# The first layer of the gate's low-rank path as three fp32r products, their low parts made on GpSimd

## The chip, the cores and the metric

The kernel runs on one core of a Trainium2 chip. Time is device time of one execution in microseconds, the median of several runs. A core has five engines with queues of their own: TensorE (PE in the profile, its weight loads PEld), VectorE (DVE), ScalarE (ACT), GpSimd (POOL) and SyncE (SP, which here issues transfers). They wait for each other at semaphores.

## What is computed

The reference is a decoder trunk of two layers over 272 tokens of 2048 features (16 learned tokens ahead of 256). Layer 0 is an RWKV-7 time mix, layer 1 a stick-breaking attention, each followed by a SwiGLU. What matters here is how the time mix makes its inputs, and one of its low-rank paths, the gate g:

```
xx = token_shift(h) - h
xr, xw, xk, xv, xa, xg = (h + xx * mu[i] for i in range(6))
r, k, v = xr @ w_r, xk @ w_k, xv @ w_v
w = -softplus(-(dec_w0 + tanh(xw @ dec_w1) @ dec_w2)) - 0.5      # dec_w1: 2048 x 96
a = sigmoid(a_w0 + (xa @ a_w1) @ a_w2)                            # a_w1:   2048 x 96
g = sigmoid(xg @ g_w1) @ g_w2                                     # g_w1:   2048 x 256
```

The change concerns the product `xg @ g_w1`.

## The kernel before, in words

Activations lie transposed in SBUF: 16 tiles of 128 features by 272 tokens, numbered k. A matrix product with a 2048-wide input sums over these 16 k in PSUM.

Most products are made in two parts. A float32 tensor is cast by ScalarE to the type fp32r (the high part) and VectorE subtracts the cast from the original (the low part). A product is then three fp32r matmuls, high by high, high weight by low activation and low weight by high activation (`mm3k`, lines 189 to 191). Weights arrive in tiles `raw` by SyncE's queue and are split so, in chunks of 512 columns, into `whi` (line 170) and `wlo` (line 171). A chunk is four k, so 12 matmuls. Four `raw` tiles exist, each with two chunks, and a `raw` is free for the next load when both chunks are split.

The split chunks go by turns into the pool `whl` (six pairs) and, in the prologue, into the pool `wx` (ten tiles, tag "w", that is five pairs).

The prologue normalizes the input (tiles `hn`), makes the key projection w_k for 16 output blocks m, and beside it everything else that needs the mixes. A mix is two instructions: ScalarE makes `u` (line 451), VectorE the mix `xi` (line 452) from hn and u. `u` has three buffers, `xi` seven. The generator `rest()` makes the value mixes, then the first layers of the three low-rank paths, then the mixes for r. From block 4 on, each key projection (`proj`) is followed by the output of the block (`key_out`: copy `kt`, square, cast and low part `hs`, and two matmuls into `kq`, line 528) and by four steps of `rest()`. So four k of the low-rank first layers belong to one key block, and the 16 k take four blocks. In each k, the paths of decay (i = 1) and iclr (i = 4) are one plain float32 matmul, with 96 columns of weights, and the gate (i = 5) two, each with 128 columns (j = 0, 1). All four are line 587 before, and their tiles in PSUM are named `lr`. These weights aren't split: `da` holds dec_w1 and a_w1 of two k, `gg` g_w1 of two k, both loaded by SyncE (line 581).

No order is written by hand here: a scheduler lays out every engine's instructions when the kernel is built, and each engine then takes its own in that order. It put each group of four k as a "burst" a few matmuls behind the start of the next key block. GpSimd does nothing in the prologue; behind it, in the scan, it fills some tiles and solves small triangles.

Of the kernel before, what the change touches and what calls it, by code (L numbers as in the profile page):

```python
# [11 lines left out]
F32 = mybir.dt.float32  # L12
F32R = mybir.dt.float32r
AF = mybir.ActivationFunctionType
ALU = mybir.AluOpType
# [3 lines left out]
NK = D // 128  # L19
META = 16  # L20
SEQ = 256
T = META + SEQ
# [99 lines left out]
class Builder:  # L122
# [286 lines left out]
    def prologue(self, hid):  # L409

        tc, nc, a = self.tc, self.nc, self.a
        V, A = nc.vector, nc.scalar
        with ExitStack() as ctx:
            x0 = ctx.enter_context(tc.tile_pool(name="x0", bufs=NK))
            wx = ctx.enter_context(tc.tile_pool(name="wx", bufs=NWX))
# [8 lines left out]
            def xtile():  # L424
                return pt.tile([128, T], F32, name="xi", tag="xi", bufs=NXL)
# [23 lines left out]
            def mixed(i, k, out):  # L449
                u = pt.tile([128, T], F32, name="u", tag="u", bufs=NSQ)  # L450
                A.mul(u, hn[k][:, :T], self.vec(f"mu{i}", k))
                V.scalar_tensor_tensor(out, hn[k][:, 1:], self.vec(f"om{i}", k), u, ALU.mult, ALU.add)

            def mix(i, k, pool):
                x = xtile()
                mixed(i, k, x)
                if pool is not self.xs2:
                    return self.split(x, pool)
                hi, lo = (pool.tile([128, T], F32R, name=n, tag="s") for n in ("hi", "lo"))
                A.copy(hi, x)  # L460
                V.tensor_tensor(lo, x, hi.bitcast(F32), ALU.subtract)
                return hi, lo
# [3 lines left out]
                                                         tag="mm" if m < 2 else "fr")  # L466
# [12 lines left out]
            for k in range(NK):  # L479
# [4 lines left out]
                x = xtile()  # L484
                mixed(2, k, x)
                for m in range(G0):
                    o = k % 4 * 128
                    nc.tensor.matmul(ps[m][:, :T], w0[m, k // 4][:, o:o + 128], x,  # L488
                                     start=k == 0, stop=k == NK - 1)
# [63 lines left out]
            def hsplit(t, name):  # L553
                m = t.shape[0]
                hi = hid.tile([m, T], F32R, name=name + "h", tag=name + "h")
                lo = hid.tile([m, T], F32R, name=name + "l", tag=name + "l")
                A.copy(hi, t)
                V.tensor_tensor(lo, t, hi.bitcast(F32), ALU.subtract)
                return hi, lo

            def rest():

                for k in range(NK):
                    self.xv.append(mix(3, k, self.xs1))
                    yield 1
                names = ((1, ["dec_w1"]), (4, ["a_w1"]), (5, ["g_w1", "g_w1"]))
                bk = {(i, j): (self.psd if i < 5 else self.pfr).tile(
                    [128, 512], F32, name="lr", tag="sd" if i < 5 else "fr")
                    for i, n in names for j in range(len(n))}
                for k in range(NK):  # L570
                    if k % 2 == 0:
                        w = {}
                        da = self.l2.tile([128, 512], F32, name="raw", tag="w2", bufs=2)
                        gg = self.l2.tile([128, 512], F32, name="raw",
                                          tag="w2h" if k % 4 else "w2l", bufs=1)
                        for (i, j), t, o, c, src in (
                                ((1, 0), da, 0, 96, a["dec_w1"]), ((4, 0), da, 192, 96, a["a_w1"]),
                                ((5, 0), gg, 0, 128, a["g_w1"][0]),
                                ((5, 1), gg, 256, 128, a["g_w1"][1])):
                            w[i, j] = t[:, o:o + 2 * c]  # L580
                            nc.sync.dma_start(w[i, j], src[:, k * c:(k + 2) * c])
                    for i, n in names:
                        x = xtile()
                        mixed(i, k, x)
                        c = 96 if i < 5 else 128
                        for j in range(len(n)):
                            nc.tensor.matmul(bk[i, j][:c, :T], w[i, j][:, k % 2 * c:k % 2 * c + c], x,  # L587
                                             start=k == 0, stop=k == NK - 1)
                    yield 1
                for i, name in ((1, "dec_w1"), (4, "a_w1")):  # L590
                    t = xtile()[:96]
                    if i == 1:
                        A.activation(t, bk[i, 0][:96, :T], AF.Tanh)
                        self.hw = hsplit(t, name)
                    else:
                        A.copy(t, bk[i, 0][:96, :T])
                        self.ha = hsplit(t, name)
                for j in range(2):
                    g = xtile()
                    A.activation(g, bk[5, j][:, :T], AF.Tanh, scale=0.5)  # L600
                    V.tensor_scalar(g, g, 0.5, 0.5, ALU.mult, ALU.add)
                    self.hg.append(hsplit(g, f"hg{j}"))
                yield 1
                for k in range(NK):
                    self.xr.append(mix(0, k, self.xs2))
                    yield 1

            g = rest()
            for m in range(G0, NK):
                key_out(m, self.proj(a["w_k"][m], xk))  # L610
# [903 lines left out]
```

## Time and profile before

| | us |
|---|---|
| median of 3 runs | 2654.6 (2654.39 to 2655.65) |
| the profiled execution | 2656.68 |
| its span, first to last instruction | 2654.9 |
| PE busy in it | 2641.9 |
| VectorE, ScalarE, GpSimd busy | 1787.6, 1490.5, 174.1 |
| the four bursts of line 587 | 82.2 to 130.4 in the span |

A row of the timeline gives start, length, engine, line, operation, out<-in and shapes; instructions of one kind in a row are merged ("x7"), and behind them stands the idle time ahead and what ended it. PE's matmuls are pipelined, so the time between starts is the cost of one, not its length. A float32 matmul stands as two records, an fp32r one as one.

### The profile page before, as it was taken

What the parts mean: (1) busy time and instruction counts of PE and PEld (TensorE: products, weight loads), DVE (VectorE), ACT (ScalarE), POOL (GpSimd) and SP (SyncE); (2) the same over time, 40 slices, a digit from 0 to 9 for tenths busy, and PEclk for the clock granted to TensorE, in tenths of its full rate; (3) what the DMA queues carried; (4) which work ended last, traced back from release to release, by engine and by line L of the source; (5) the groups of instructions that cost most, each with busy time, mean ns of one, the idle gap of its engine ahead of it and who ended that gap; (6) DMA issues with size and microseconds to landing.
All of it is one profiled execution on the core that took longest, in us unless ns stands there. A gap on an engine that the chain in (4) does not pass through costs nothing.

```text
span 2654.9 us, 54070 instructions
## 1 busy us (share of the span) xinstructions
PE 2641.9 (100%) x20966; PEld 2455.2 (92%) x20966; DVE 1787.6 (67%) x3618; ACT 1490.5 (56%) x3017; POOL 174.1 (7%) x493
## 2 busy tenths in 40 slices
PE   9999999999999999999999999999999999999999
PEld 8898888889999999999999999888888888888888
DVE  7677777766655555555557775788766666666665
ACT  7775666666544444444446764676555455554553
POOL 0014343440000000000000000000000000000000
PEclk9999999999999999999999999999999999999999
DMA  6434343445555555555555555434555655665655
GB/s 229 145 120 130 96 127 97 124 132 165 174 175 165 186 175 165 185 176 167 184 174 168 181 167 175 143 120 137 189 187 180 197 188 176 201 190 176 199 180 177
DMA packets 186385, 439.54 MB, mean 166 GB/s; under 512 B 58736, under 2 KB 89616, under 8 KB 186128
## 3 DMA queue, kind: packets, MB, share of 16 engines
q1 hardware_dynamic: 184784, 432.90, 51.9%
q8 instruction: 164, 2.69, 0.4%
q0 software_dynamic: 768, 2.23, 0.3%
q10 hardware_dynamic: 576, 0.96, 0.1%
q14 instruction: 93, 0.76, 0.1%
HBM read 430.28 MB, written 5.74 MB: 164 GB/s over the span
## 4 chain that ended last, share of the span: by engine, by line
PE 97%; DMA 1%; ACT 1%; issue 1%; DVE 0%; POOL 0%; SPq 0%; POOLq 0%; ACTq 0%
PE mm L194 23%; PE mm L189 17%; PE mm L191 17%; PE mm L190 17%; PE mm L193 12%; PE lr L587 1%; PE mm L488 1%; PE cb L1426 1%; PE zb L1363 1%; PE yb L1344 1%; PE wa L1374 1%; PE z L1054 1%; PE cb L1418 0%; PE lt L1067 0%; PE ba L1226 0%
## 5 line engine op out<-in xcount | busy, mean ns | idle before, releaser
L171 DVE TENSOR_TENSOR wlo<-raw,whi 128x512 fp32r<-128x512 f32 (+1 forms) x1432 | 968.0, 679 | 596.4 <-ACT whi L170 576.5
L170 ACT CAST whi<-raw 128x512 fp32r<-128x512 f32 (+1 forms) x1432 | 870.3, 610 | 841.2 <-PE mm L190 531.3
L189 PE MATMUL mm<-hl,whi 128*128 128x272 f32 x3328 | 967.2, 291 | 0.0
L191 PE MATMUL mm<-hl,wlo 128*128 128x272 f32 x3328 | 960.4, 289 | 0.0
L190 PE MATMUL mm<-hl,whi 128*128 128x272 f32 x3328 | 958.1, 288 | 0.0
L194 PE MATMUL mm<-hl,whi 128*128 128x512 f32 x2624 | 919.9, 394 | 0.0
L193 PE MATMUL mm<-hl,wlo 128*128 128x256 f32 x2624 | 738.1, 282 | 0.0
L189 PEld LDWEIGHTS mm<-hl,whi 128*128 128x128 f32 x3328 | 625.3, 188 | 10.7 <-issue 8.1
L190 PEld LDWEIGHTS mm<-hl,whi 128*128 128x128 f32 x3328 | 631.2, 190 | 0.0
L191 PEld LDWEIGHTS mm<-hl,wlo 128*128 128x128 f32 x3328 | 625.6, 188 | 0.2
L194 PEld LDWEIGHTS mm<-hl,whi 128*128 128x128 f32 x2624 | 492.4, 188 | 111.9
L193 PEld LDWEIGHTS mm<-hl,wlo 128*128 128x128 f32 x2624 | 494.3, 188 | 0.3
L218 DVE TENSOR_TENSOR wlo<-raw,whi 128x512 fp32r<-128x512 f32 (+2 forms) x156 | 106.6, 691 | 21.7 <-ACT whi L217 19.3
L217 ACT CAST whi<-raw 128x512 fp32r<-128x512 f32 (+2 forms) x156 | 93.1, 609 | 41.4 <-PE mm L190 40.9
L210 DVE TENSOR_TENSOR h<-h,mm 128x256 f32<-128x256 f32 (+1 forms) x224 | 93.9, 420 | 6.6 <-PE mm L194 6.0
L203 ACT COPY c<-mm 128x256 f32<-128x256 f32 x104 | 38.8, 373 | 75.8 <-PE mm L194 75.8
L1281 POOL TENSOR_TENSOR Ts<-Ts,Tm 40x14 f32<-40x14 f32 (+6 forms) x224 | 76.6, 342 | 17.6
L189 PE MATMUL mm<-hi,whi 128*128 128x272 f32 x256 | 75.5, 295 | 0.0
L1279 POOL TENSOR_TENSOR Tm<-Ts,As 40x14 f32<-40x14 f32 (+6 forms) x224 | 74.3, 331 | 17.5
L190 PE MATMUL mm<-lo,whi 128*128 128x272 f32 x256 | 73.8, 288 | 0.0
L191 PE MATMUL mm<-hi,wlo 128*128 128x272 f32 x256 | 73.4, 287 | 0.0
L189 PEld LDWEIGHTS mm<-hi,whi 128*128 128x128 f32 x256 | 48.0, 188 | 1.1
(295 smaller groups left out, 2365.1 us busy)
## 6 DMA issues: line engine op xcount, KB each, us to landing
raw<-w_gate SPq DMA_DIRECT2D x176, 512.0 KB
raw<-w_up SPq DMA_DIRECT2D x176, 512.0 KB
raw<-w_down SPq DMA_DIRECT2D x128, 512.0 KB
raw<-w_down SPq DMA_DIRECT2D x128, 192.0 KB
raw<-w_v SPq DMA_DIRECT2D x32, 512.0 KB
raw<-w_r SPq DMA_DIRECT2D x32, 512.0 KB
raw<-sb_w_k SPq DMA_DIRECT2D x32, 512.0 KB
raw<-sb_w_v SPq DMA_DIRECT2D x32, 512.0 KB
```

Of the source, the lines that this page charges most:

```text
L170: nc.scalar.copy(hi, part)
L171: nc.vector.tensor_tensor(lo, part, hi.bitcast(F32), ALU.subtract)
L189: mm(out, w[0], x[0], start=first, stop=False)
L190: mm(out, w[0], x[1], start=False, stop=False)
L191: return mm(out, w[1], x[0], start=False, stop=last)
L193: mm(out[:, :n], w[1], x[0], start=first, stop=False, skip_group_check=True)
L194: return mm(out, w[0], x[2], start=False, stop=last, skip_group_check=True)
L210: self.nc.vector.tensor_tensor(h, h, out[:, c:c + n], ALU.add)
L217: self.cast = nc.scalar.copy(hi, part)
L218: nc.vector.tensor_tensor(lo, part, hi.bitcast(F32), ALU.subtract)
L1279: V.tensor_tensor(t, Ts[:, 0:i, i:i + 1].to_broadcast([40, i, n]), As[:, i:i + 1, i + 1:].to_broadcast([40, i, n]), ALU.mult)
L1281: V.tensor_tensor(Ts[:, 0:i, i + 1:], Ts[:, 0:i, i + 1:], t, ALU.add)
```

## The change

The two gate products of each k become six fp32r matmuls. The weights `gg` of two k are split once into `gh` (ScalarE) and `gl` (GpSimd), two tiles from the pool `wx`. The gate's mix is split into `gxh` (ScalarE) and `gxl` (GpSimd), two tiles from the pool `xs2`. Decay and iclr stay as they were; their line is now 600.

```
                             w[i, j] = t[:, o:o + 2 * c]
                             nc.sync.dma_start(w[i, j], src[:, k * c:(k + 2) * c])
+                        gh, gl = (wx.tile([128, 512], F32R, name=s, tag="w") for s in ("gh", "gl"))
+                        A.copy(gh, gg)
+                        nc.gpsimd.tensor_tensor(gl, gg, gh.bitcast(F32), ALU.subtract)
                     for i, n in names:
                         x = xtile()
                         mixed(i, k, x)
-                        c = 96 if i < 5 else 128
+                        if i == 5:
+                            xh, xl = (self.xs2.tile([128, T], F32R, name=s, tag="s") for s in ("gxh", "gxl"))
+                            A.copy(xh, x)
+                            nc.gpsimd.tensor_tensor(xl, x, xh.bitcast(F32), ALU.subtract)
+                            for j in range(2):
+                                o = j * 256 + k % 2 * 128
+                                for q, (u, v) in enumerate(((gh, xh), (gl, xh), (gh, xl))):
+                                    nc.tensor.matmul(bk[i, j][:, :T], u[:, o:o + 128], v,
+                                                     start=k + q == 0, stop=k == NK - 1 and q == 2)
+                            continue
+                        c = 96
                         for j in range(len(n)):
                             nc.tensor.matmul(bk[i, j][:c, :T], w[i, j][:, k % 2 * c:k % 2 * c + c], x,
                                              start=k == 0, stop=k == NK - 1)
```

The scheduler lays out other engines' rows anew with it. ScalarE in the second burst, from the copy `kt` of the key block ahead of it (u are mixes, xi here the square, hs its cast, whi a key weight), before:

```order
L499 COPY kt_1161<-mm_1112 128x272
L504 ACTIVATE xi_1163<-kt_1161,vecs_65 128x272
L507 CAST hs_1165<-xi_1163 128x272
L451 ACTIVATE u_1193<-hn_97,vecs_65 128x272
L451 ACTIVATE u_1198<-hn_97,vecs_65 128x272
L170 CAST whi_1566<-raw_1564 128x512
L451 ACTIVATE u_1203<-hn_97,vecs_65 128x272
L451 ACTIVATE u_1215<-hn_98,vecs_65 128x272
L451 ACTIVATE u_1220<-hn_98,vecs_65 128x272
L451 ACTIVATE u_1225<-hn_98,vecs_65 128x272
```

Now the same place on ScalarE:

```order
L499 COPY kt_1201<-mm_1152 128x272
L170 CAST whi_1720<-raw_1714 128x512
L504 ACTIVATE xi_1203<-kt_1201,vecs_65 128x272
L451 ACTIVATE u_1245<-hn_97,vecs_65 128x272
L507 CAST hs_1205<-xi_1203 128x272
L451 ACTIVATE u_1250<-hn_97,vecs_65 128x272
L590 CAST gxh_1234<-xi_1230 128x272
L451 ACTIVATE u_1255<-hn_97,vecs_65 128x272
L451 ACTIVATE u_1279<-hn_98,vecs_65 128x272
L451 ACTIVATE u_1284<-hn_98,vecs_65 128x272
L583 CAST gh_1468<-raw_1463 128x512
L590 CAST gxh_1258<-xi_1254 128x272
```

The key weight's cast has moved ahead of the square and a mix ahead of the cast hs; casts of the gate's mix and weights stand among the mixes.

PE at the start of the second burst (lr_1012 decay, lr_1013 iclr, lr_1014 and lr_1015 the gate's two halves), before:

```order
L587 MATMUL lr_1012<-xi_1176,raw_1170 96x272
L528 MATMUL kq_461<-hs_1165,selr_458 128x272
L587 MATMUL lr_1013<-xi_1181,raw_1170 96x272
L528 MATMUL kq_461<-hs_1165,selr_458 128x272
L587 MATMUL lr_1014<-xi_1186,raw_1171 128x272
L587 MATMUL lr_1015<-xi_1186,raw_1171 128x272
L587 MATMUL lr_1012<-xi_1192,raw_1170 96x272
L587 MATMUL lr_1013<-xi_1197,raw_1170 96x272
```

Now the same place on PE:

```order
L600 MATMUL lr_1012<-xi_1220,raw_1210 96x272
L600 MATMUL lr_1013<-xi_1225,raw_1210 96x272
L528 MATMUL kq_461<-hs_1205,selr_458 128x272
L189 MATMUL mm_1346<-hl_312,whi_1332 128x272
L600 MATMUL lr_1012<-xi_1244,raw_1210 96x272
L528 MATMUL kq_461<-hs_1205,selr_458 128x272
L595 MATMUL lr_1014<-gxh_1234,gh_1216 128x272
L595 MATMUL lr_1014<-gxh_1234,gl_1217 128x272
L595 MATMUL lr_1014<-gxl_1235,gh_1216 128x272
L595 MATMUL lr_1015<-gxh_1234,gh_1216 128x272
L595 MATMUL lr_1015<-gxh_1234,gl_1217 128x272
L595 MATMUL lr_1015<-gxl_1235,gh_1216 128x272
```

The gate's products stand behind a decay product of the next k, and the third of them takes GpSimd's gxl, with three more behind it in PE's order.

GpSimd, which had no row here before, now has these from the start of the second burst on (gl of the third burst among them, each ahead of a gxl):

```order
L584 TENSOR_TENSOR gl_1411<-raw_1405,gh_1410 128x512
L591 TENSOR_TENSOR gxl_1235<-xi_1230,gxh_1234 128x272
L584 TENSOR_TENSOR gl_1469<-raw_1463,gh_1468 128x512
L591 TENSOR_TENSOR gxl_1259<-xi_1254,gxh_1258 128x272
L591 TENSOR_TENSOR gxl_1293<-xi_1288,gxh_1292 128x272
L591 TENSOR_TENSOR gxl_1317<-xi_1312,gxh_1316 128x272
```

All eight low parts of weights are made a burst or more ahead of their use, the mixes' low parts inside the burst.

## The prediction

> **What bounds the kernel now.** I read the page's busy times and its chain that ended last, and then asked for the stage in which the changed lines run.
>
> ```profile
> span 2654.9 us, 54070 instructions
> PE 2641.9 (100%) x20966; PEld 2455.2 (92%) x20966; DVE 1787.6 (67%) x3618; ACT 1490.5 (56%) x3017; POOL 174.1 (7%) x493
> PE 97%; DMA 1%; ACT 1%; issue 1%; DVE 0%; POOL 0%; SPq 0%; POOLq 0%; ACTq 0%
> ```
>
> TensorE (PE) is busy all the time and is 97% of the chain, so a shorter or longer stretch on PE should move the end by as much. The changed products (line 587, tile lr) are windows of the prologue, four "bursts" of four k each, one behind the start of each of four key projections. The busy time by window (stretch: sum, PE busy, PEld busy, clock, DMA share, GB/s), the pieces of the chain (start, us) and the waits between 80 and 136 us (total, times, longest) show them:
>
> ```profile
> 82.15:89.62 7.47, 7.47 (x32) 5.46 (x32) 1.00 0.52 139
> 95.20:102.71 7.51, 7.51 (x32) 5.36 (x32) 1.00 0.50 168
> 122.90:130.40 7.50, 7.50 (x32) 5.36 (x32) 1.00 0.32 109
> 96.61 6.46 PE lr L587 x28
> ACT whi L170 <- PE mm L190: 19.0, 12, 3.0
> PEld lr L587 <- DVE xi L452: 1.2, 6, 0.2
> ```
>
> A burst takes 7.5 us and PE waits in it only 1.2 us in all. But that is close: ScalarE and VectorE feed it in the same seconds. The timelines of the second burst (start, us, engine, line) have the pace of every feeding step:
>
> ```profile
> 93.92 0.38 ACT L499 COPY kt<-mm 128x272 f32<-128x272 f32 x1
> 94.33 0.52 ACT L504 ACTIVATE xi<-kt,vecs 128x272 f32<-128x272 f32 x1
> 94.89 0.42 ACT L507 CAST hs<-xi 128x272 fp32r<-128x272 f32 x1
> 95.21 0.93 ACT L451 ACTIVATE u<-hn,vecs 128x272 f32<-128x272 f32 x2
> 96.05 0.60 ACT L170 CAST whi<-raw 128x512 fp32r<-128x512 f32 x1
> 96.56 1.34 ACT L451 ACTIVATE u<-hn,vecs 128x272 f32<-128x272 f32 x3
> 98.20 3.00 ACT L451 ACTIVATE u<-hn,vecs 128x272 f32<-128x272 f32 x7 [0.30 <-DVE xi L452]
> 95.48 0.44 DVE L508 TENSOR_TENSOR hs<-xi,hs 128x272 fp32r<-128x272 f32 x1
> 95.83 1.32 DVE L452 SCALAR_TENSOR_TENSOR xi<-hn,dv,u 128x272 f32<-128x272 f32 x3
> 97.06 0.69 DVE L171 TENSOR_TENSOR wlo<-raw,whi 128x512 fp32r<-128x512 f32 x1
> 97.67 2.98 DVE L452 SCALAR_TENSOR_TENSOR xi<-hn,dv,u 128x272 f32<-128x272 f32 x7
> ```
>
> Start to start: a mix costs ScalarE 0.42 us and VectorE 0.42 us (7 in 3.0), a 128x272 cast 0.32, a 128x512 cast 0.51, a wlo 0.61.
>
> **What the change takes from PE.** An old product is two records: 28 in 6.46 us, 0.461 us a product. An fp32r product starts every 0.125 us: first and last of 37 rows of PE's timeline, 4.49 us over 36 steps:
>
> ```profile
> 77.53 0.29 PE L190 MATMUL mm<-hl,whi 128*128 128x272 f32 x1
> ...
> 82.02 0.29 PE L190 MATMUL mm<-hl,whi 128*128 128x272 f32 x1
> ```
>
> Each of the 32 gate products becomes three: 0.461 - 0.375 = 0.086 us, 0.69 us a burst, 2.75 us in all. That is everything the change can win. The 64 added weight loads are hidden as the key projection's are, whose pace of 0.125 already holds one load a matmul.
>
> **What it adds.** ScalarE: 16 casts of 0.32 and 8 of 0.51, 9.2 us. GpSimd (POOL): 16 subtractions of 128x272 and 8 of 128x512. No row of before has these sizes; the nearest are the ones of 40x256 and 40x14 (count, busy and mean ns), and two pairs that met a VectorE operation with two SBUF inputs:
>
> ```profile
> L1274 POOL TENSOR_TENSOR Ts<-As,consts 40x256 f32<-40x256 f32 x16 | 13.3, 829 | 221.5 <-DMA As<-s 187.5 <-issue 34.0
> L1279 POOL TENSOR_TENSOR Tm<-Ts,As 40x14 f32<-40x14 f32 x32 | 8.1, 252 | 2.5
> 411.75 0.68 DVE L218 TENSOR_TENSOR wlo<-raw,whi 128x512 fp32r<-128x512 f32 x1
> 411.77 1.26 POOL L1274 TENSOR_TENSOR Ts<-As,consts 40x256 f32<-40x256 f32 x1 [12.95 <-DMA As<-s]
> 253.45 0.73 POOL L1274 TENSOR_TENSOR Ts<-As,consts 40x256 f32<-40x256 f32 x1 [14.10 <-DMA As<-s]
> 253.59 1.14 DVE L218 TENSOR_TENSOR wlo<-raw,whi 128x512 fp32r<-128x512 f32 x1
> ```
>
> In the first pair VectorE began 0.02 us earlier and kept its 0.68; GpSimd ended 0.60 after it. In the second GpSimd was first and kept its 0.73; VectorE ended 0.55 after that and so took 1.14. Each holds the other up for a whole operation. Scaled by size, a gxl (128x272) holds the path 0.63 us behind a VectorE operation and a gl (128x512) 0.60 and 256 elements more at 2.0 ns ((730 - 252)/242) to 2.4 ns ((829 - 252)/242): 1.11 to 1.21, 1.15 taken. The ends: nothing at all if mixes don't collide; 0.88 and 1.66 by the mean of 829 ns. I take 0.63 and 1.15, since the pairs show the collision itself. The mix is a SCALAR_TENSOR_TENSOR, which no row of before shows beside GpSimd.
>
> [...]
>
> **The second burst, walked.** Zero is the start of the key copy (93.92 before). The new order puts the cast of a key weight ahead of the square, a mix ahead of the hs cast, and a gh cast into the burst. ScalarE: copy 0, weight cast 0.41, square 0.92, mix 1.48, hs cast 1.90 to 2.32, mix, gxh_1234 from 2.64 to 3.05. PE reaches its first burst product at 1.28 (95.20), has two products without gate done at 2.20, waits 0.2 for hs and 0.1 for the next mix, and has the two gate products that use no gxl done at 3.45. GpSimd could start gxl_1235 at 3.1, but VectorE is in a mix to 3.30, so it ends at 3.93: PE waits 0.5. VectorE, held until 3.93, does wlo to 4.50 and two mixes to 5.30; GpSimd then takes gl_1469 to 6.45, VectorE a mix to 6.85, GpSimd gxl_1259 to 7.50. PE stands ready for that at 6.1: it waits 1.45. gxl_1293 ends at 9.4 (PE waits 0.25), gxl_1317, behind three more mixes, at 11.3 (0.5), and the burst at 11.75. Without waits it is 1.28 + 8 x 0.461 + 24 x 0.125 + 0.25 (two key sums) + 0.5 (four key products that now lie inside) = 8.72, so PE waits 3.0. Before, it ended at 1.28 + 7.51 = 8.79; less those 0.5, the burst is 2.46 us longer.
>
> **The sum.** Third burst: the same order, 2.46. First: its gl is at the same place (gl_1275), but no wlo lies in it, 0.6 less: 1.9. Fourth: no gl is left, 1.15 less: 1.3. Ahead of the first burst both feeding engines are nearly full (stretch, then PE, PEld, DVE, ACT, POOL):
>
> ```profile
> 60.00:82.00 22.00, 21.99 (x172) 21.34 (x171) 20.80 (x47) 21.48 (x53) 0.00 (x0) 1.00 0.49 163
> ```
>
> By the order, four gh casts stand there in place of five weight casts, so ScalarE has less to do; VectorE loses five wlo (3.0) and is held up by four gl (4.6), 1.6 more in a stretch in which it has 1.2 idle: 0.4 is left. Sum: 0.4 + 1.9 + 2.46 + 2.46 + 1.3 = +8.5 us. Against the profiled execution (2656.7, its span 2654.9) that is 2665.2; it stands 2.1 above the median of the runs, 2654.6, which becomes 2663.1.
>
> At nothing I cost: gh and gl taking up to 8 of the 10 extra weight buffers (the key weights are split as soon as PE frees a buffer, 19.0 us of waiting, 11 pairs of 1.5 us ahead; seven are left); the g_w1 loads, which go ahead on SyncE's queue because GpSimd now frees their buffer, and hold the w_k loads behind them until a gl is done (the same cover of 10 us); GpSimd's memsets for the scan, queued behind the last gxl, which run 20 us later. If the cover goes, a late w_k load stops ScalarE just behind the key copy (the cast named above), and with it the whole burst: that is the fourth case.
>
> **The rivals.** One, gain kept: everything added is hidden, 2654.6 - 2.75 = 2651.9, not slower. It decides if the last gxl of each burst is ready when PE comes to it. Against it: ScalarE alone, with nothing colliding, runs copy 0.41, weight cast 0.51, square 0.56, hs 0.32, 11 mixes of 0.42, gh 0.51 and four gxh of 0.32, to 8.2; then gxl 0.78 (0.73 by size) and 0.5 of products: 9.5 against 8.72.
> Two, only TENSOR_TENSOR collides and mixes don't: the wait is that of ScalarE's row, 0.8, and some 0.3 behind gl: 1.1 a burst, 4.4 in all, 2654.6 + 4.4 - 2.75 = 2656.3. For it: no row with a mix. Against it: mix and wlo both read two SBUF tensors.
> Three, worse: GpSimd at its mean (0.25 more a gxl, 0.5 more a gl, 1.5 us a burst where both lie in it, 5 in all) or w_k loads late: 2654.6 + 8.5 + 5.5 = 2668.6.
>
> **How the numbers follow.** Collision as walked, 0.57 (its own range 2659.5 to 2666.5: the first and the last burst at half or at the full price); only ScalarE's row, 0.20; gain kept, 0.08; worse, 0.15. The range from 2655.5 to 2669.5 leaves out the kept gain, half of the worse case and a little more, 0.19. 0.2%, about what a measurement can tell from no change, is 5.3 us: slower is above 2659.9. That takes most of the walked case (0.49) and all of the worse one, 0.63 with rounding; the rest is within it, 0.35; faster than 2649.3 needs twice the whole gain, 0.02.
>
> **What will show it.** Right, if lr's fp32r products wait for gxl from GpSimd, some 2 to 3 us a burst and most in the second and third; if mixes last up to 1.1 us where a GpSimd operation runs, and GpSimd's 128x272 over 0.8; if bursts go from 7.5 to some 10 to 10.5 us on PE. Wrong, if GpSimd's operations take their time beside unhurt mixes, if PE waits at ScalarE's casts or at key weights (whi) instead, or if the scan behind the prologue gives time back.

## The result and the profile after

The changed kernel takes 2666.6 us (median of 6 runs, 2665.22 to 2667.88), the kernel before beside it 2655.1 us (2653.99 to 2658.24). The ratio is 1.0043 with an interval of 1.0033 to 1.0053: it is slower by 0.33 to 0.53%. By the medians that is 11.5 us more. The profiled execution took 2665.82 us, 9.1 more than the profiled one of before.

From the page of the changed kernel, span and busy times:

```profile
span 2664.1 us, 54204 instructions
PE 2643.7 (99%) x20998; PEld 2456.2 (92%) x20998; DVE 1801.2 (68%) x3618; ACT 1501.2 (56%) x3041; POOL 203.1 (8%) x517
```

PE is busy only 1.8 us longer, although the end comes 9.2 us later: what was added is waiting. Where it came in is shown by the copies `kt` (start, length), which mark the end of every key block. Before:

```profile
67.21 0.38 ACT L499 COPY kt<-mm 128x272 f32<-128x272 f32 x1
73.74 0.38 ACT L499 COPY kt<-mm 128x272 f32<-128x272 f32 x1
80.17 0.37 ACT L499 COPY kt<-mm 128x272 f32<-128x272 f32 x1
93.92 0.38 ACT L499 COPY kt<-mm 128x272 f32<-128x272 f32 x1
107.78 0.38 ACT L499 COPY kt<-mm 128x272 f32<-128x272 f32 x1
121.61 0.38 ACT L499 COPY kt<-mm 128x272 f32<-128x272 f32 x1
135.45 0.38 ACT L499 COPY kt<-mm 128x272 f32<-128x272 f32 x1
```

And after:

```profile
67.11 0.38 ACT L499 COPY kt<-mm 128x272 f32<-128x272 f32 x1
75.25 0.38 ACT L499 COPY kt<-mm 128x272 f32<-128x272 f32 x1
81.69 0.37 ACT L499 COPY kt<-mm 128x272 f32<-128x272 f32 x1
100.22 0.39 ACT L499 COPY kt<-mm 128x272 f32<-128x272 f32 x1 [1.02 <-PE mm L191]
115.74 0.39 ACT L499 COPY kt<-mm 128x272 f32<-128x272 f32 x1 [1.00 <-PE mm L191]
131.04 0.39 ACT L499 COPY kt<-mm 128x272 f32<-128x272 f32 x1 [0.99 <-PE mm L191]
146.28 0.38 ACT L499 COPY kt<-mm 128x272 f32<-128x272 f32 x1
```

The block that ends at 73.74, where no burst lies, is 1.6 us longer (8.14 against 6.53). The four blocks with bursts took 13.75, 13.86, 13.83 and 13.84 us; now they take 18.53, 15.52, 15.30 and 15.24: 4.78, 1.66, 1.47 and 1.40 more. At 146.28 the kernel is 10.8 us late; behind the prologue 1.6 of that come back.

The four bursts by window (stretch: sum, PE, PEld, DVE, ACT, POOL busy, clock, DMA share, GB/s) took 7.5 us each before. PE now stands still in them for 2.75, 1.43, 1.43 and 0.96 us (sum less PE busy), and in the first the granted clock is 0.86. Behind them stand the weight loads' waits between 55 and 150 us (total, times, longest), which show a stall whole, where a matmul's modelled end hides some of it:

```profile
84.32:96.16 11.84, 9.09 (x44) 7.50 (x45) 8.13 (x14) 7.70 (x18) 7.63 (x5) 0.86 0.22 56
101.52:111.70 10.18, 8.75 (x50) 6.81 (x49) 7.90 (x12) 8.96 (x22) 4.99 (x5) 1.00 0.27 83
117.05:127.02 9.97, 8.54 (x50) 6.82 (x49) 7.82 (x12) 8.67 (x22) 4.94 (x5) 1.00 0.08 23
132.35:141.96 9.61, 8.65 (x51) 6.96 (x50) 7.53 (x14) 8.48 (x22) 3.98 (x4) 1.00 0.34 106
PEld lr L595 <- POOL gxl L591: 8.7, 10, 3.0
PEld kq L528 <- ACT hs L507: 2.1, 8, 0.5
PEld kq L528 <- DVE hs L508: 1.6, 1, 1.6
PEld lr L600 <- DVE xi L452: 1.2, 1, 1.2
```

That is 13.6 us; the same table of before has two rows, hs 1.2 and xi 1.2. So 11.2 us of waiting were added. Less the 2.75 that the products save by the prediction's sum, that is 8.4 of the 10.8 us. Of the other 2.4, the slower clock of the first burst accounts for some 1.6 (worked out below, where PE is kept busy); 0.8 stay open.

Three places of the timeline show how the waits arise. The longer block without a burst: a gl on GpSimd, the low part hs on VectorE behind it, and PE's key sum behind that.

```profile
69.10 1.35 POOL L584 TENSOR_TENSOR gl<-raw,gh 128x512 fp32r<-128x512 f32 x1 [1.75 <-ACT gh L583]
69.24 1.50 DVE L508 TENSOR_TENSOR hs<-xi,hs 128x272 fp32r<-128x272 f32 x1
70.80 0.40 PE L528 MATMUL kq<-hs,selr 128*128 128x272 f32 x1 [1.35 <-DVE hs L508]
```

hs takes 0.44 us when alone; here GpSimd was 0.14 us earlier, hs took 1.50, and PE had hs next in its order. The first burst, with a window of what followed:

```profile
83.44 5.19 POOL L584 TENSOR_TENSOR gl<-raw,gh 128x512 fp32r<-128x512 f32 x1 [0.81 <-ACT gh L583]
85.37 3.56 DVE L452 SCALAR_TENSOR_TENSOR xi<-hn,dv,u 128x272 f32<-128x272 f32 x6
88.59 2.60 POOL L591 TENSOR_TENSOR gxl<-xi,gxh 128x272 fp32r<-128x272 f32 x3
89.60 0.39 PE L595 MATMUL lr<-gxl,gh 128*128 128x272 f32 x1 [2.75 <-POOL gxl L591]
90.20:92.90 2.70, 2.70 (x12) 2.24 (x11) 1.70 (x3) 1.90 (x5) 1.46 (x3) 0.51 0.37 104
```

This gl takes 5.19 us, four times what the others do (median 1.32). It began behind a wlo of VectorE, whose operations then followed each other without a gap until about 87.5. It isn't wanted yet: it is gl_1275, the weights of k = 6 and 7, which belong to the second burst. But the first burst's gxl stand behind it on GpSimd's queue. PE waits 2.75 us, and then works for about 3.4 us at half its clock (half-microsecond windows read 0.50 from 90.5 to 93.5). The second burst is as the prediction has it:

```profile
104.69 5.00 DVE L452 SCALAR_TENSOR_TENSOR xi<-hn,dv,u 128x272 f32<-128x272 f32 x7
105.19 1.54 POOL L584 TENSOR_TENSOR gl<-raw,gh 128x512 fp32r<-128x512 f32 x1 [0.97 <-ACT gh L583]
106.70 0.96 POOL L591 TENSOR_TENSOR gxl<-xi,gxh 128x272 fp32r<-128x272 f32 x1
107.70 0.39 PE L595 MATMUL lr<-gxl,gh 128*128 128x272 f32 x1 [1.10 <-POOL gxl L591]
```

Seven mixes take 5.00 us, 2.98 before. By group between 80 and 150 us (busy, mean ns), mixes before, mixes after, and gxl:

```profile
L452 DVE SCALAR_TENSOR_TENSOR xi<-hn,dv,u 128x272 f32<-128x272 f32 x58 | 25.3, 494 | 0.0
L452 DVE SCALAR_TENSOR_TENSOR xi<-hn,dv,u 128x272 f32<-128x272 f32 x48 | 27.8, 623 | 8.5 <-ACT u L451 7.3 <-POOL gxl L591 0.7
L591 POOL TENSOR_TENSOR gxl<-xi,gxh 128x272 fp32r<-128x272 f32 x16 | 14.2, 895 | 20.8 <-ACT gxh L590 20.0 <-PE lr L595 0.8
```

### The profile page after: what moved, and what is told of

Same layout as the page of the kernel before. It is cut to its first block, busy times and chain, and to the rows that moved or that the text cites. A ratio compares the mean times of both kernels' runs of the same rounds, so it can differ in the third digit from the quotient of the medians.

```text
span 2664.1 us, 54204 instructions
## 1 busy us (share of the span) xinstructions
PE 2643.7 (99%) x20998; PEld 2456.2 (92%) x20998; DVE 1801.2 (68%) x3618; ACT 1501.2 (56%) x3041; POOL 203.1 (8%) x517
## 4 chain that ended last, share of the span: by engine, by line
PE 95%; ACT 2%; POOL 1%; DVE 1%; DMA 1%; issue 1%; SPq 0%; ACTq 0%; DVEq 0%; POOLq 0%
PE mm L194 23%; PE mm L189 17%; PE mm L191 16%; PE mm L190 16%; PE mm L193 12%; PE mm L488 1%; PE cb L1439 1%; PE zb L1376 1%; PE yb L1357 1%; PE wa L1387 1%; PE cb L1431 1%; PE z L1067 1%; PE lt L1080 0%; PE ba L1239 0%; PE hms L988 0%
## 5 line engine op out<-in xcount | busy, mean ns | idle before, releaser
L452 DVE SCALAR_TENSOR_TENSOR xi<-hn,dv,u 128x272 f32<-128x272 f32 x96 | 50.0, 559 | 8.5 <-ACT u L451 7.3
```

## The experiments

The theory: GpSimd and VectorE hold each other up, and PE waits for what is late by it. The rival: the longer row of ScalarE and of the feeding steps, whoever subtracts. The scheduler lays out all engines' rows anew for each of these kernels, so a difference between two of them can hold a change of order too; only where GpSimd reads one tensor did it keep the changed kernel's order (but for three swaps of neighbours on PE). In the first four runs the kernel before had 2656.1 us, in the next four 2655.7, in the last three 2654.8.

**Both low parts on VectorE.**

```
-nc.gpsimd.tensor_tensor(gl, gg, gh.bitcast(F32), ALU.subtract)
+V.tensor_tensor(gl, gg, gh.bitcast(F32), ALU.subtract)
-nc.gpsimd.tensor_tensor(xl, x, xh.bitcast(F32), ALU.subtract)
+V.tensor_tensor(xl, x, xh.bitcast(F32), ALU.subtract)
```

> Both low parts, gl and gxl, on VectorE; GpSimd has nothing in the prologue, ScalarE's and TensorE's work is that of the changed kernel. Theory (GpSimd and VectorE hold each other up, and TensorE waits for the late gxl): most of the +11.5 us goes. VectorE's two 128x512 subtractions go back to 0.69 us and its mixes to 0.42 to 0.49; a burst then costs VectorE 12 mixes of 0.42, four gxl of 0.44, two gl of 0.69, a wlo and an hs, 9.2 us, about what TensorE needs (8.7), so some waiting is left: 0.5 to 4 us over the kernel before (2655.5 to 2659). No stretch of a burst has a granted clock under 0.9. Rival (the extra casts on ScalarE and the number of steps alone make a burst longer, whoever subtracts): still 8 us or more slower than before, with TensorE waiting for gxh or for mixes.

2658.5 us, ratio 1.0007 (0.9998 to 1.0016): no difference from before can be told. The blocks took 12.92, 14.13, 13.34 and 14.43 us, and the block ahead of them 6.51; the profiled execution, 2655.5 us, is among the three shortest of eleven, which lie some 3 us below the rest. Most of the loss goes with GpSimd, although ScalarE still has all its casts and VectorE has 24 more operations. The rival, which had 8 us or more, is out.

**One of the two on VectorE.** The same two lines, first gl alone, then gxl alone.

> Only gl moves to VectorE; gxl stays on GpSimd. Theory that one starved gl (5.19 us in the first burst) and the slower clock behind it make the first burst's excess: the first block (key copy to key copy, 18.53 us in the changed kernel, 13.75 before) comes down to 15 to 15.5, the lead-in's 1.5 us goes, and the other three stay 1 to 1.5 over before: 4 to 6.5 us over before in all (2659 to 2661.5). Rival (gxl does it, gl is no matter): 9 to 11 us over before, first block over 17.5.

> Only gxl moves to VectorE; gl stays on GpSimd. If gl behind back-to-back two-input operations of VectorE is what costs: the first gl of a burst is late again, first block 16.5 to 18.5 us, and the others 0.5 to 1 over before, 6 to 10 us over before in all. If the 16 gxl are what costs: 1 to 4 us over before.

gl on VectorE: 2664.3 us, ratio 1.0033 (1.0021 to 1.0046). The longer block ahead of the bursts is gone (6.51), as expected, but the first burst's block still takes 16.52 us and the time is 8 us over before, between the theory's 4 to 6.5 and the rival's 9 to 11. A row each of GpSimd and of PE, and a window:

```profile
84.21 4.33 POOL L591 TENSOR_TENSOR gxl<-xi,gxh 128x272 fp32r<-128x272 f32 x2 [83.76 <-ACT gxh L590]
87.86 0.39 PE L595 MATMUL lr<-gxl,gh 128*128 128x272 f32 x1 [2.89 <-POOL gxl L591]
86.00:88.00 2.00, 0.14 (x1) 0.14 (x2) 1.34 (x4) 1.05 (x3) 2.00 (x2) 1.00 0.48 130
```

Now it is the first gxl that is shut out: VectorE goes without a gap from 84.26 (gl, mixes, wlo, mix) to 87.19, and the first gxl is there only after that. In both kernels what stood on GpSimd in that stretch was late: a gl of 5.19 us there, a gxl of 3.60 here.

gxl on VectorE: 2663.2 us, ratio 1.0028 (1.0017 to 1.0040), within what was expected, but not in the place: the blocks took 14.43, 18.36, 14.75 and 13.97 us. The profiled execution, 2666.2 us, is the longest of its six. GpSimd's row, SyncE's wait between 82 and 103 us, what followed on ScalarE and on PE, and a window:

```profile
83.90 7.91 POOL L584 TENSOR_TENSOR gl<-raw,gh 128x512 fp32r<-128x512 f32 x1 [0.81 <-ACT gh L583]
SPq L581 <- POOL gl L584: 9.5, 3, 7.2
100.72 0.62 ACT L170 CAST whi<-raw 128x512 fp32r<-128x512 f32 x1 [3.75 <-DMA raw<-w_k]
102.53 0.55 PE L528 MATMUL kq<-hs,selr 128*128 128x272 f32 x1 [3.56 <-ACT hs L507]
103.00:104.00 1.00, 1.00 (x5) 0.73 (x3) 1.00 (x4) 1.00 (x4) 0.00 (x0) 0.50 0.00 0
```

The gl was shut out for 7.91 us. SyncE's load of the next gate weights waited for its buffer, the key weights' loads stood behind that load, and in the second burst ScalarE waited 3.75 us for them with the square and hs behind it. This is the prediction's case of late w_k loads, with its price: 4.5 us in one block.

**PE kept busy while it waits.**

```
+if k == 0:
+    for _ in range(24):
+        nc.tensor.matmul(bk[5, 0][:, 272:512], gh[:, :128], xh[:, :240],
+                         start=True, stop=True, skip_group_check=True)
```

> The changed kernel with 24 products more (fp32r, 240 columns, into a part of the bank that nothing reads) ahead of the first gate product, so that TensorE isn't idle while it waits for the late gl and gxl of the first burst. Theory that the idle time takes the granted clock down (0.51 over 2.7 us behind it): the clock stays at 1.0 in the first burst, its block is 1.2 to 1.5 us shorter than the changed kernel's 18.53, and the kernel about 10 us over before instead of 11.5. Rival (the clock falls for another reason, or the slow stretch is hidden behind ScalarE and VectorE): block still 18.5, or longer if the added products outlast the wait.

2664.9 us, ratio 1.0036 (1.0022 to 1.0050). The clock stayed at 1.00 in the burst, and the gl took 5.22 us again. The first block took 17.93 us, 0.6 less than in the changed kernel. The burst itself gained more: from the first product that waits for gxl to the next key product it took 5.16 us (89.77 to 94.93), in the changed kernel 6.79 (89.60 to 96.39). So the slow clock had cost some 1.6 us there. The block shows only 0.6 of it, because the new order on ScalarE has a key weight ahead of the key copy that ends the block, and that weight came late:

```profile
98.71 0.62 ACT L170 CAST whi<-raw 128x512 fp32r<-128x512 f32 x1 [3.03 <-DMA raw<-w_k]
```

By the medians, 8.8 us over before against 11.5, with intervals that overlap, the gain isn't shown.

**GpSimd reads one tensor only.**

```
-nc.gpsimd.tensor_tensor(gl, gg, gh.bitcast(F32), ALU.subtract)
+nc.gpsimd.tensor_copy(gl, gg)
-nc.gpsimd.tensor_tensor(xl, x, xh.bitcast(F32), ALU.subtract)
+nc.gpsimd.tensor_copy(xl, x)
```

> The changed kernel with GpSimd copying (gl from raw, gxl from the mix: one tensor read, the low parts are not formed) instead of subtracting; every engine has the changed kernel's order. Theory that it is two-input operations on both engines that hold each other up: the copies run in their own time, mixes stay at 0.42 to 0.49, TensorE's waits for gxl go below 1.5 us in all, and the kernel ends between 2.75 us faster and 2 us slower than before. Rival (any GpSimd operation on SBUF is held by VectorE's two-input ones, or GpSimd is just slow): a copy in the first burst takes 4 to 5 us again, and the kernel is 6 to 12 us slower.

2657.7 us, ratio 1.0009 (1.0000 to 1.0018). GpSimd's row in the first burst, and the mixes between 80 and 150 us:

```profile
81.39 4.46 POOL L584 CAST gl<-raw 128x512 fp32r<-128x512 f32 x1 [2.05 <-PE mm L191]
L452 DVE SCALAR_TENSOR_TENSOR xi<-hn,dv,u 128x272 f32<-128x272 f32 x55 | 26.4, 519 | 8.9 <-ACT u L451 8.5 <-POOL gxl L591 0.3
```

Half of each side. The copy is shut out for 4.46 us, as the rival had it; but VectorE is hardly held up any more (mixes 519 against 623 ns, wlo at most 694), and a copy is shorter (gxl 507 ns in the mean), so the loss is nearly gone. PE still waits 1.7 us for one gxl. A block now takes 15.29 us at most. Since the copies' own length fell too, the run doesn't part the two effects.

**VectorE reads one tensor at a time.**

```
-V.scalar_tensor_tensor(out, hn[k][:, 1:], self.vec(f"om{i}", k), u, ALU.mult, ALU.add)
+V.tensor_scalar(out, u, 0.5, 0.5, ALU.mult, ALU.add)
+V.tensor_scalar(out, out, 0.5, 0.5, ALU.mult, ALU.add)
```

> The changed kernel, but each of VectorE's mixes is two TENSOR_SCALAR that read one tensor each (the term with hn is left out of the mix), about as long in sum as the mix; GpSimd's subtractions are as they were. Theory that only a two-tensor operation of VectorE shuts GpSimd out: the first gl of the first burst takes 1.3 to 2 us instead of 5.19, TENSOR_SCALAR stay at 0.28 to 0.30, and the first block comes down to 15 us or less. Rival (any float32 operation of VectorE on SBUF does, as the 1.31 us of one kqr suggests): gl over 3 us again, some TENSOR_SCALAR of over 1 us.

One run, 2669.1 us; its order is another and its row on VectorE has more latency, so only the lengths are read. The last two gl ahead of the first burst's gxl, and VectorE between them:

```profile
80.84 1.48 POOL L585 TENSOR_TENSOR gl<-raw,gh 128x512 fp32r<-128x512 f32 x1 [6.80 <-DVE kqr L661]
81.09 1.38 DVE L662 TENSOR_SCALAR kqr<-kqr 32x272 f32<-32x272 f32 x1
83.08 1.58 POOL L585 TENSOR_TENSOR gl<-raw,gh 128x512 fp32r<-128x512 f32 x1 [0.76 <-ACT gh L584]
83.47 1.56 DVE L452 TENSOR_SCALAR xi<-u 128x272 f32<-128x272 f32 x2
```

Again each theory has a half. gl takes 1.58 us where it took 5.19, so here, at one place of one run, a row of one-tensor operations let GpSimd in. But GpSimd holds these operations up too: kqr takes 1.38 us, 0.28 in the kernel before, where GpSimd has nothing, and of the two at 83.47 one takes over a microsecond. The first block, 16.71 us, didn't come down to 15.

**All is made, nothing of it is used.** gh, gl, gxh and gxl are made; PE does the plain products:

```
-for q, (u, v) in enumerate(((gh, xh), (gl, xh), (gh, xl))):
-    nc.tensor.matmul(bk[i, j][:, :T], u[:, o:o + 128], v, start=k + q == 0, stop=k == NK - 1 and q == 2)
+nc.tensor.matmul(bk[i, j][:, :T], gg[:, o:o + 128], x, start=k == 0, stop=k == NK - 1)
```

> The changed kernel's casts and GpSimd subtractions are all made, but TensorE uses the plain float32 gate products as before (so nothing waits for gxh, gxl, gh or gl, and the 2.75 us are not won). Theory (GpSimd also hurts through VectorE, whose mixes and hs are held up): TensorE waits for mixes and hs instead, 1 to 2.5 us a burst and 1.3 ahead of the first: 4 to 9 us slower than before. Rival (only the direct wait of the products for gxl costs): within 1.5 us of before.

2661.0 us, ratio 1.0025 (1.0014 to 1.0036). Though no product waits for GpSimd, 5.3 us are lost. Between 55 and 150 us PE waits for three things that VectorE makes (and 0.4 us for a key weight of ScalarE), and ScalarE waits for the gate's weights:

```profile
PE kq L528 <- DVE hs L508: 1.3, 1, 1.3
PE mm L191 <- DVE wlo L171: 1.3, 3, 0.9
PE lr L594 <- DVE xi L452: 0.7, 3, 0.3
ACT gh L583 <- DMA raw<-g_w: 7.2, 4, 2.4
```

The theory's time holds, but not all of it is VectorE's. That wlo, the key weights' low part, comes late as well was not expected, and in part it comes late because of the last row: in this kernel's order key weights stand on ScalarE behind a gh that waits for its load, which the changed kernel doesn't have. So the run shows that the direct wait isn't the only cost; it doesn't give VectorE's share.

**Products four k behind their split**, with the low parts on GpSimd and then on VectorE (the six matmuls stand in a function `gate`):

```
-                            for j in range(2):
-                                ...
+                            pend.append((k, gh, gl, xh, xl))
+                            if len(pend) > 4:
+                                gate(*pend.pop(0))
                             continue
...
+                while pend:
+                    gate(*pend.pop(0))
```

> The changed kernel with the gate's products issued four k later than their split (one key block later), so a gxl has some 13 us until TensorE wants it; GpSimd still makes both low parts. Theory that TensorE's direct wait for gl and gxl is the larger part, and VectorE's held-up mixes the smaller: waits for gxl go, no clock drop, blocks 14 to 15 us, and 0 to 5 us slower than before. If the mixes are the larger part: 5 to 9 us slower.

> As the run before, but both low parts on VectorE: nothing of GpSimd left, and no product close behind its split. If the gain of 0.086 us a product is there to be had: 0 to 2.75 us faster than before (2652 to 2654.6 where before is 2654.6). If VectorE's 12 us of added subtractions come ahead of mixes: 0 to 3 us slower.

With GpSimd: 2660.8 us, ratio 1.0022 (1.0013 to 1.0031), 5.1 us over before, at the edge of what was expected. No product waits for gxl, but the block ahead of the bursts takes 8.16 us again, PE waits 2.7 us for mixes and 3.1 for hs, and ScalarE 10.4 us for key weights, with SyncE's queue held by gl for 11.3. So distance takes away the direct wait, and the two others remain.

With VectorE: 2653.8 us, ratio 0.9992 (0.9984 to 1.0001). Once more, and with a distance of two k:

> The same kernel as lag4_vector once more, to narrow its interval (2653.8 against 2655.7 before it). If the 32 gate products' 0.086 us each are won and nothing else is lost: 1.5 to 2.75 us faster, ratio 0.9990 to 0.9994. If the first result was chance: within 1 us.

> Both low parts on VectorE and the gate's products two k behind their split (half a key block), so fewer products are left over behind the last block than with four. If the distance of four is more than is needed: the same as lag4_vector, 1.5 to 2.75 us faster than before. If VectorE's row needs the longer distance: between that and the kernel without distance, 0 to 2 us slower than before.

2654.2 and 2654.1 us, each with a ratio of 0.9997 (0.9988 to 1.0006), against 2654.8 before: 0.6 and 0.7 us. Four k behind gave 1.9 us once and 0.6 once, less than expected the second time. Measured against the kernel before beside each, these kernels beat the changed one by some 12 us. That they beat the one before isn't shown. In the profile of the first, PE waits 1.7 us for hs by its own rows, which show no wait before (the weight loads' rows have 3.9 against 1.2); that may be where the rest of the 2.75 went.

## Why the prediction was right, and where it wasn't

Slower was forecast, at 2663.1 us and between 2655.5 and 2669.5; 2666.6 lies in that, though by the medians it is 11.5 us slower and not 8.5. The profiled execution was forecast at 2665.2 and took 2665.8. That this is so close is luck: the lead-in and the first burst were forecast 4.0 us too short, the second and third 1.8 too long, and 1.6 came back behind the prologue.

- **Mechanism.** Right: products wait for gxl, mixes take up to 1.52 us, gxl 0.90 in the mean, bursts 9.6 to 10.2 us but for the first, 11.8. Not so: most of the waiting was to be in the second and third burst, and the first had the most. That both low parts on VectorE undo most of the loss shows that it is GpSimd. That mixes collide, which no row of before showed, is so.
- **The gain of 2.75 us.** Its price holds where PE doesn't wait: the last k of the changed kernel's first burst, two plain and six fp32r products, takes 1.69 us (94.70 to 96.39), 1.67 by the sum and 1.84 for four plain products. In the time it isn't shown. The kernels with both low parts on VectorE and a distance of two or four k are 0.6 to 1.9 us faster than before, none beyond the measurement's interval; the one without distance isn't faster.
- **Lead-in, 0.4 forecast, 1.5 measured.** The step compared what VectorE has to do with the time it has. But a single operation was enough: hs, next in PE's order, 0.14 us behind a gl. A wait is read from the order at the place, not from the stretch's idle sum. The sum also counted four gl there, and three lay in it; the fourth is the first burst's own (83.44), which the sum counts again there.
- **First burst, 1.9 forecast, 4.8 measured.** The step that failed is that the engines take turns. Both pairs of rows it drew on were single operations; here VectorE had a row without a gap (83.18 to 87.50), and the gl got in at its end. The walk also priced this gl at its own length, where it holds four gxl behind it on its queue. The slower clock behind the wait added some 1.6 us and was not thought of.
- **Second and third, 2.46 forecast, 1.66 and 1.47 measured.** The walk holds in its middle: gxl_1259 ended 7.44 us behind the key copy (107.66 less 100.22), 7.50 walked. It ran long at the end: the last gxl came at 10.78, not 11.3, and the key product behind the burst at 11.31, not 11.75. Measured alike, from the first product of the burst to the second key product behind it, the second burst takes 10.14 us (101.52 to 111.66) against 7.83 before (95.20 to 103.03). That is 2.31 more, 1.81 without the four key products that moved in (0.5), and close to the block's 1.66.
- **Fourth, 1.3 forecast, 1.40 measured.** Right.
- **Key weights at nothing.** Right in this kernel (ScalarE waited 0.2 us for them), by little: with gxl on VectorE, with PE kept busy, and with the products four k behind on GpSimd's low parts, the cover was gone.
- **Behind the prologue.** Nothing was forecast, and time given back by the scan was named as a sign of being wrong. In the profiled executions 1.6 of 10.8 us come back. The place can be seen: in the same work PE stands still for 2.3 us of 34 before, and for 0.3 us of 33 in the changed kernel:

```profile
188.00:222.00 34.00, 31.68 (x430) 28.13 (x430) 21.64 (x54) 16.41 (x46) 15.24 (x45) 1.00 0.37 111
199.00:232.00 33.00, 32.71 (x445) 29.15 (x443) 22.86 (x56) 17.39 (x49) 14.45 (x43) 1.00 0.42 119
```

The profiles of the other eleven runs, early or late at that place, also lose 1.0 to 2.7 us less there than the profile of before, so it may lie in that one execution of before. By the medians, 11.5 us, nothing comes back.

## What to carry to other kernels

Moving a subtraction to an idle GpSimd wasn't free here, where VectorE works on two-tensor operations (11.5 us over before, 2.4 with both low parts on VectorE): look in the timeline for rows of VectorE without a gap, since a gl here got in only behind one (5.19 us), and for the VectorE operation that PE wants next, since it may stand behind a whole GpSimd operation as hs did (1.50 us behind a gl of 1.35). On GpSimd's queue put what is wanted first ahead of what is wanted later, and ask which load on another queue waits for its buffers. A saving of 0.1% of the time isn't worth a new dependence between two engines in a stretch that both nearly fill.

## What was not expected of the hardware

In the first burst GpSimd was shut out for as long as VectorE's two-tensor operations followed each other (83.18 to 87.50): 5.19 us for a 128x512 subtraction that took 1.29 where VectorE stood idle (at 99.27). With PE kept busy it took 5.22 us there, with gxl on VectorE 7.91, and a copy of one tensor 4.46. With one-tensor operations on VectorE it took 1.58, at one place of one run. Of single pairs, one operation stood behind the whole of the other (hs 1.50 us behind a gl of 1.35). Nor was a row without a gap the same everywhere: in the first burst the gl got no turn between two operations of VectorE, in the second one did, between two mixes at 105.11 and 105.52 (the gl took 1.54 us, the mix behind it 1.52). What decides between the two is not shown.

A wait of 2.75 us was followed by 3.41 us at half clock (90.23 to 93.64), one of 3.56 us (gxl on VectorE) by a clock of 0.50 too, but one of 2.89 us (gl on VectorE) by none: its clock reads 1.00 throughout. So the length of the wait alone doesn't decide; what does is not shown. With PE kept busy the clock reads 1.00 from 84 to 98.
